# Late sort passes, group sizes and clear widths in a scatter-add kernel

## The chip, the cores and the metric

The kernel runs on one core of one Trainium2 chip. The metric is the device time of one launch in microseconds (us). The engines are PE (matmuls), PEld (its weight loads), DVE (elementwise work on vectors), ACT (activations and copies), POOL (here mostly the issuing of DMAs) and SP (issuing DMAs). Each engine takes its own instructions in order and waits on semaphores for the others.

## The reference

```python
N, E, D = 4096, 262144, 256
self_out = nodes @ w_self
src_feat = nodes[edges_src]          # E x D
msg = src_feat @ w_msg
agg = np.zeros((N, D)); np.add.at(agg, edges_dst, msg)
return self_out + agg
```

The edges are drawn once at random (uniform sources and destinations), the same draw each time.

## The kernel before

The kernel does not gather rows. It uses that the sum over edges is A @ (nodes @ w_msg), where A[dst, src] counts edges. `Y = nodes @ w_msg` is made once; A is made piece by piece in PSUM by matmuls of one-hot matrices and is multiplied by Y.

**Sort.** Every edge becomes a key: a destination segment (11 segments of SW = 374 destinations), then a source block (32 blocks of 128 sources), then the destination, then the source. One segment with one block is a *run* (NRUN = 352). DVE sorts the 262144 keys nearly, with a fixed list of compare-exchange passes (`SORT_A`, then 16 last passes `SORT_S`, each a minimum and a maximum). The sorted keys are cut into 2048 *chunks* of 128. The first 1024 chunks are the early half, the other 1024 the late half (HALF = 1024). Of the late half the 32 instructions of `SORT_S` are put off (`sort.late`): they run on DVE between the groups of the counting loop.

**Counting loop** (line 560 on). For each chunk one matmul adds e^T d into a PSUM bank: e is 128 edges by 128 sources, one-hot; d is 128 edges by W = 110 destinations, one-hot, at a column offset that PE reads from a register (`poff`). The offset is where the chunk's lowest destination lies in its run (`dl`). DVE makes e and d for a *group* of chunks at a time (`onehots`, list `sizes`): one subtraction `e_off` (L396), eight comparisons `e_oh` (L402), then `d_off` and seven `d_oh`. Each tile of one-hots has three buffers, so DVE may be up to three groups ahead.

**Ring.** The runs use six PSUM banks in turn. Before a run, `clear(r)` writes zeros with one matmul into GAP columns at each end of the SW + W = 484 columns of its bank; the columns between must then be covered by the chunks' windows. After a run ACT evicts the bank to SBUF as bf16 (L481); the last 110 columns, which belong to the start of the next run, are added to that run's tile by a DMA that POOL issues (`merge`, L501, two runs at a time), or are multiplied by an extra matmul (L519). 46 chunks later three matmuls (L524) multiply the run by its block of Y. At the end of a segment ACT copies the result and SP stores it in 12 pieces, one for every second eviction (L611).

**Late half.** Once its passes are done (chunk LATE_SUB), `late.bases()` finds each late chunk's lowest destination on DVE, `late.subtract` makes relative keys, `turn_late(0)` and `turn_late(1)` transpose them on PE through a bank slot of the ring that is set aside at run SHIFT (the second at chunk LATE_TURN), with an activation on ACT after each, and `late.places()` computes the offsets. `split_vals` then splits the values for the one-hots of chunk 1024 on.

**Order.** The order of everything up to `order.__exit__` is written out by hand. The check after it (L615 on) is placed among it by the scheduler: each half's `k16` is stored to a small DRAM row `kd` and loaded again shifted by one chunk as `kn`, both on SP's queue; `gn`, `v`, `bad` on DVE compare neighbours; a matmul (L642) sums them, and the result decides whether a plain loop (`_any_edges`) does the work anew.

The late passes go into the loop by this piece of before:

```python
if c >= LATE_FROM:
    for _ in range(LATE_STEP):
        if rest:
            rest.pop(0)()
if c == LATE_SUB:
    assert not rest
    late.bases()
```

Of the kernel before, what the change touches and what calls it, by code (L numbers as in the profile page):

```python
# [16 lines left out]
ALU = mybir.AluOpType  # L17
# [3 lines left out]
BW = 512  # L21
SW = 374
W = 110
GAP = W - 8
NB = 32
JB = 16
HALF = 1024
SHIFT = 148
LATE_FROM = 256
LATE_STEP = 4  # L30
LATE_SUB = 768
LATE_TURN = 872
LATE_USE = 960
NSEG = 11
NRUN = NSEG * NB
OFF = 6 * (NB - 1)
# [47 lines left out]
def kernel(  # L84
# [14 lines left out]
    NCOL = E // P  # L99
# [28 lines left out]
    tss = nc.vector.tensor_single_scalar  # L128
    tt = nc.vector.tensor_tensor
    stt = nc.vector.scalar_tensor_tensor  # L130
# [50 lines left out]
    for (c0, c1), (d64, s64) in zip(PIECES, ld):  # L181
        dlo = d64[:].bitcast(I32)[:, 0::2]
        slo = s64[:].bitcast(I32)[:, 0::2]
        c = slice(c0, c1)
# [3 lines left out]
            out=seg[:, c], in_=dlo, func=ACTF.Copy, scale=1.0 / SW, bias=0.5 / SW - 6.5  # L188
        )
        loaded = nc.scalar.activation(  # L190
            out=blk[:, c], in_=slo, func=ACTF.Copy, scale=1.0 / P, bias=0.5 / P - 0.5
# [62 lines left out]
    sort = _Sort(nc, tc, psum_sort, XA, (XS, XL), id2, zw)  # L254
    own = sort.run(plan, halo, project)

    def col16(name, dt):
        return meta.tile([P, G16], dt, name=name)

    k16, kmin, kn, rho, rhoc, gi, gn, dl, sl, wr, poff = (  # L260
        col16(n, I32)
        for n in ("k16", "kmin", "kn", "rho", "rhoc", "gi", "gn", "dl", "sl", "wr", "poff")
    )
# [7 lines left out]
    class Half:  # L271
# [47 lines left out]
        def places(self):  # L319
# [6 lines left out]
            if self.h == 0:  # L326
                stt(
                    out=sl[:, c], in0=rhoc[:, c], scalar=float(SHIFT - OFF), in1=sl[:, c],
                    op0=ALU.is_ge, op1=ALU.add,
# [44 lines left out]

    split_at = {0: 64, 64: 512, 512: HALF, HALF: HALF + 256, HALF + 256: NCOL}

    sizes = [8, 8, 16, 32, 32, 32] + [64] * ((NCOL - 128) // 64)
    assert sum(sizes) == NCOL

    def onehots(c, n):  # L380
# [32 lines left out]
    def clear_at(r):  # L413
        return min(max(line(at, r) for at in CLEAR[0:3]), line(CLEAR[3], r))

    def evac_at(r):
        return min(line(at, r + 1) for at in EVAC)
# [6 lines left out]
    def count_mm(ap, lhsT, rhs, start, after=()):  # L424
        mm = nc.tensor.matmul(  # L425
            out=ap, lhsT=lhsT, rhs=rhs, start=start, stop=True, skip_group_check=True,
        ).ins
        tc.declare_no_dep(
            mm, group="evac", keep=after, reason="disjoint banks by static schedule"
        )  # L430
        for i in after:
            tc.add_manual_dep(mm, i.name, DEP, reason="bank free")
        tc.add_to_no_dep_group("count", mm)
        last_mm[0] = mm
        return mm

    def bank(r):
        return (r + (r >= SHIFT)) % RING * BW

    def bank_free(slot):  # L440

        old = slot - RING
        if old == SHIFT:
            return [late_read[-1]]
        return [evac_of[old - (old > SHIFT)]] if old >= 0 else []

    late_read = []

    def turn_late(t):
        b = bank(SHIFT - 1) // BW  # L450
        b = (b + 1) % RING * BW
        mms, act = late.turn(t, ring[:, b:b + BW])
        for m in mms:
            after = bank_free(SHIFT) if t == 0 else [late_read[-1]]
            tc.declare_no_dep(
                m.ins, group="evac", keep=after, reason="disjoint banks by static schedule"
            )
            for i in after:
                tc.add_manual_dep(m.ins, i.name, DEP, reason="bank free")
            tc.add_to_no_dep_group("count", m.ins)  # L460
        ins = act.ins
        tc.declare_no_dep(
            ins, group="count", keep=[m.ins for m in mms], reason="disjoint banks by static schedule"
        )
        tc.add_manual_dep(ins, mms[-1].ins.name, DEP, reason="transposed")
        tc.add_to_no_dep_group("evac", ins)
        late_read.append(ins)

    def clear(r):
        b = bank(r)  # L470
        after = bank_free(r + (r >= SHIFT))
        zone = bass.AP(
            tensor=ring.tensor, offset=ring[:, b:b + 1].offset,
            ap=[list(ring[:].ap[0]), [SW + W - GAP, 2], [1, GAP]],
        )
        count_mm(zone, zer[:, 0, :], zer[:, 1:3, 0:GAP], True, after)

    def evac(r):
        at = ats[r % NAT]
        b = bank(r)  # L480
        ins = nc.scalar.copy(out=at[:, 0:SW + W], in_=ring[:, b:b + SW + W]).ins  # L481
        tc.declare_no_dep(
            ins, group="count", keep=[last_mm[0]], reason="disjoint banks by static schedule"
        )
        tc.add_manual_dep(ins, last_mm[0].name, DEP, reason="run complete")
        tc.add_to_no_dep_group("evac", ins)
        evac_of[r] = ins
        at_of[r] = at
# [4 lines left out]
    def by_dma(r):  # L493
        return r < NRUN - 8 and r // 2 % 6 > 0

    def merge(r):

        i, j = r % NAT, (r + 1) % NAT
        pairs = [(i, j, 2)] if j + 2 <= NAT else [(i, j, 1), (j, 0, 1)]
        for a, b, n in pairs:  # L500
            nc.gpsimd.dma_start(  # L501
                out=atr[:, b:b + n, 0:W], in_=atr[:, a:a + n, SW:SW + W], accum_op=ALU.add
            )
# [45 lines left out]
    if True:  # L549
        todo = []  # L550
        regs = []
        ncl = 0
        nev = 0
        rest = sort.late
        starts = {}
        c = 0
        for n in sizes:
            starts[c] = n
            c += n
        for c in range(NCOL):  # L560
            if c in starts:
                c0 = c
                if c == LATE_USE:
                    late.places()
                e, d = onehots(c, starts[c])
                if c >= LATE_FROM:
                    for _ in range(LATE_STEP):
                        if rest:
                            rest.pop(0)()
                if c == LATE_SUB:  # L570
                    assert not rest
                    late.bases()
                    for t in range(2):
                        late.subtract(t)
            if c == LATE_TURN:
                turn_late(1)
                late.total()
            ci = c - c0
            while ncl < NRUN and clear_at(ncl) <= c:
                if ncl == SHIFT:  # L580
                    turn_late(0)
                clear(ncl)
                ncl += 1
            if c % 8 == 0:
                regs = [nc.tensor.alloc_register(f"po{c}_{i}") for i in range(8)]
                q, h8 = c % HALF // G8, c // HALF * G8
                nc.tensor.load(regs, poff[q:q + 1, h8:h8 + 8])
            addr = nc.tensor.snap(
                regs[c % 8], donate=True, min_val=PSUM0, max_val=PSUM0 + 4 * (RING * BW - W)
            ).with_bounds(  # L590
                min_val=PSUM0, max_val=PSUM0 + 4 * (RING * BW - W),
                guaranteed_mod_val=0, out_of_modulus=4,
            )
            off = (addr - PSUM0) // 4
            count_mm(
                ring[:, bass.ds(off, W)], e[:, ci // 2, :, ci % 2], d[:, ci // 2, :, ci % 2], False
            )
            for _ in range(FILL.get(c + 1, 0)):
                nc.tensor.matmul(  # L599
                    out=out_ps[:, 2:4, :], lhsT=zw[:, 0:P], rhs=zw[:], start=True, stop=True,  # L600
                    skip_group_check=True,
                )
            while nev < NRUN and (evac_at(nev) <= c or c == NCOL - 1):
                evac(nev)
                if nev % 2 == 0 and nev and by_dma(nev - 1):
                    merge(nev - 2)
                todo.append((c + LAG + (SWITCH if nev % NB == 0 else 0), nev))
                if nev % 2 and stores:
                    dst, src = stores.pop(0)
                    tc.add_manual_dep(  # L610
                        nc.sync.dma_start(dst, src).ins, evac_of[nev].name, DEP, reason="pace"  # L611
                    )
                nev += 1
            while todo and (todo[0][0] <= c or c == NCOL - 1):
                apply_run(todo.pop(0)[1])  # L615
# [3 lines left out]
    bad = meta.tile([P, G16], FP32, name="bad")  # L619
    v = meta.tile([P, G16], FP32, name="v")  # L620
# [7 lines left out]
    for h in range(2):  # L628
# [4 lines left out]
    tss(out=gn[:], in_=kn[:], scalar=7, op=ALU.arith_shift_right)  # L633
    tt(out=bad[:], in0=rho[:], in1=rhoc[:], op=ALU.not_equal)
    tt(out=v[:], in0=gn[:], in1=gi[:], op=ALU.subtract)
    stt(out=bad[:], in0=v[:], scalar=float(GAP), in1=bad[:], op0=ALU.is_gt, op1=ALU.add)
    stt(
        out=bad[0:1, 0:1], in0=gi[0:1, 0:1], scalar=float(GAP - 1 - SW * OFF), in1=bad[0:1, 0:1],
        op0=ALU.is_gt, op1=ALU.add,
# [358 lines left out]
```

## Time and profile before

| | |
|---|---|
| median of 6 runs | 483.83 us (482.06 to 485.62) |
| profiled execution, its own time | 482.41 us |
| its span, first to last instruction | 480.6 us |
| mean granted clock of PE | 0.961 |
| busy: PE, DVE, ACT, POOL | 376.9, 416.0, 240.6, 196.3 us |
| first count matmul, last count matmul | 167.02, 469.51 us |
| clear matmuls of 128x204 | 352 of them, mean 251 ns each |
| late passes (XL, L746) | 32 of them, 28.1 us busy |

Times in the trace are us from the span's start. A line of a timeline gives start, length, engine, line of the kernel, operation, the tiles written and read with their shapes, and the number of like instructions; in brackets stand the idle time before and what ended it. Matmuls overlap in the array, so that the distance between two starts, not the length of one, is what a matmul costs PE. The page's span and the profiled execution's own time differ by what lies around the first and the last instruction.

### The profile page before, as it was taken

How to read it: one execution, taken by the hardware profiler on the slowest of the kernel's cores; microseconds unless marked ns; L12 is line 12 of the kernel's file. 1: busy time of each engine (PE TensorE's matmuls, PEld its weight loads, DVE VectorE, ACT ScalarE, POOL GpSimd, SP SyncE). 2: the span in 40 equal slices, each digit the busy share in tenths (PEclk: the TensorE clock that was granted, in tenths of full speed). 3: DMA queues.
4: the chain of work that ended last, by engine and by line, in shares of the span. 5: the costliest groups of instructions: out<-in, count | busy, mean ns of one | idle time of the engine just before them, and what ended most of it. 6: DMA issues, size and time to landing. Idle time of an engine off the chain costs nothing.

```text
span 480.6 us, 10985 instructions
## 1 busy us (share of the span) xinstructions
PE 376.9 (78%) x4098; PEld 309.2 (64%) x4107; DVE 416.0 (87%) x884; ACT 240.6 (50%) x459; POOL 196.3 (41%) x190
## 2 busy tenths in 40 slices
PE   0009636989872798987987997899998999999994
PEld 0004231655441368986877987789997999898893
DVE  8999999899899999999999998999987797987400
ACT  3100010321282245775555666677776777677771
POOL 4200000000000035765554566477666676766760
PEclk9999986999997799999899999999999999999998
DMA  8794111111000013343333334344544454544451
GB/s 324 114 165 131 25 26 25 28 25 25 14 0 0 2 14 26 30 51 38 28 41 38 32 30 54 37 47 48 49 45 49 40 57 37 56 38 53 38 60 40
DMA packets 66307, 23.78 MB, mean 49 GB/s; under 512 B 52171, under 2 KB 64971, under 8 KB 66251
## 3 DMA queue, kind: packets, MB, share of 16 engines
q0 software_dynamic: 43872, 10.42, 26.7%
q1 hardware_dynamic: 21548, 10.42, 8.2%
q10 hardware_dynamic: 830, 2.20, 1.2%
q8 instruction: 34, 0.56, 0.5%
q14 instruction: 23, 0.18, 0.1%
HBM read 8.92 MB, written 6.30 MB: 32 GB/s over the span
## 4 chain that ended last, share of the span: by engine, by line
DVE 42%; PE 34%; POOL 7%; issue 7%; DMA 6%; ACT 2%; SPq 0%; DVEq 0%; POOLq 0%; ACTq 0%
DVE XA L749 16%; PE ring L425 13%; PE out_ps L524 11%; DVE e_oh L402 7%; POOL atr L501 7%; DVE d_oh L402 6%; DVE XS L749 6%; PE warm L786 5%; DMA atr<-atr 4%; DVE XL L746 4%; PE tp_sw L892 2%; DMA d<-in_edges_dst_dram 2%; DVE d_off L396 1%; DVE e_off L396 1%; PE out_ps L599 1%
## 5 line engine op out<-in xcount | busy, mean ns | idle before, releaser
L501 POOL DMA_DIRECT2D atr<-atr x163 | 187.6, 1263 | 261.6 <-ACT atr L481 259.2
L481 ACT CAST atr<-ring 128x484 bf16<-128x484 f32 x352 | 192.4, 565 | 103.0 <-PE ring L425 82.7
L425 PE MATMUL ring<-d_oh,e_oh 128*128 128x110 bf16 x2048 | 195.5, 215 | 19.9 <-DVE d_oh L402 16.7
L425 PEld LDWEIGHTS <-e_oh 128*128 128x128 bf16 x2048 | 163.6, 98 | 24.9 <-issue 15.3
L524 PE MATMUL out_ps<-Y,atr 128*128 128x256 bf16 x1056 | 171.5, 274 | 2.2 <-DMA atr<-atr 1.9
L402 DVE TENSOR_SCALAR e_oh<-e_off 128x1024 bf16<-128x1024 int16 (+1 forms) x264 | 99.6, 448 | 19.5 <-PE ring L425 17.3
L786 PE MATMUL warm<-zw 128*128 128x512 bf16 x169 | 54.3, 416 | 67.4 <-DVE XA L749 51.9
L749 DVE TENSOR_TENSOR XA<-XA 128x510 f32<-128x510 f32 (+35 forms) x142 | 97.1, 732 | 5.3 <-ACT XA L896 3.6
L524 PEld LDWEIGHTS <-atr 128*128 128x128 bf16 x1056 | 90.4, 97 | 9.3 <-DMA atr<-atr 2.6
L425 PE MATMUL ring<-zer 128*128 128x204 bf16 x352 | 88.3, 251 | 1.5 <-ACT atr L481 1.3
L402 DVE TENSOR_SCALAR d_oh<-d_off 128x1024 bf16<-128x1024 int16 (+3 forms) x231 | 86.0, 442 | 1.1
L786 PEld LDWEIGHTS <-zw 128*128 128x128 bf16 x176 | 16.7, 102 | 101.1 <-issue 54.8
L896 ACT COPY XA<-tp_sw 128x512 f32<-128x512 f32 x24 | 14.2, 592 | 92.4 <-PE tp_sw L892 91.7
L425 PEld LDWEIGHTS <-zer 128*128 128x128 bf16 x352 | 34.3, 98 | 9.6 <-issue 6.0
L749 DVE TENSOR_TENSOR XS<-XS 128x512 f32<-128x512 f32 (+17 forms) x40 | 28.9, 769 | 2.6 <-ACT XS L950 2.0
L746 DVE TENSOR_TENSOR XL<-XL 128x1196 f32<-128x1196 f32 (+15 forms) x32 | 28.1, 919 | 0.3
L892 PEld LDWEIGHTS tp_sw<-XA,id 128*128 128x128 f32 x192 | 22.4, 190 | 4.6 <-issue 2.4
L892 PE MATMUL tp_sw<-XA,id 128*128 128x128 f32 x192 | 23.8, 276 | 1.9 <-DVE XA L749 1.7
L396 DVE TENSOR_TENSOR e_off<-slo_b,jrow 128x1024 int16<-128x1024 int16 (+1 forms) x33 | 21.6, 655 | 0.0
L396 DVE TENSOR_TENSOR d_off<-rel_b,drow 128x1024 int16<-128x1024 int16 (+1 forms) x33 | 21.5, 653 | 0.0
L643 DVE COPY bsum<-ring 1x3 f32<-1x3 f32 x1 | 0.1, 149 | 24.4 <-PE ring L642 24.4
L519 PE MATMUL out_ps<-Y,atr 128*128 128x256 bf16 x65 | 17.6, 271 | 0.0
(104 smaller groups left out, 153.9 us busy)
## 6 DMA issues: line engine op xcount, KB each, us to landing
atr<-atr POOLq DMA_DIRECT2D x123, 55.0 KB, 2.8
out_dram<-o_sb SPq DMA_DIRECT2D x110, 32.0 KB, 1.6
nodes_bf<-in_nodes_dram POOLq DMA_DIRECT2D x1, 2048.0 KB, 16.4
nodes_bf_dram<-nodes_bf SPq DMA_DIRECT2D x1, 2048.0 KB
atr<-atr POOLq DMA_DIRECT2D x40, 27.5 KB, 2.9
s<-in_edges_src_dram ACTq DMA_DIRECT2D x2, 512.0 KB
d<-in_edges_dst_dram SPq DMA_DIRECT2D x2, 512.0 KB, 8.2
XT<-nodes_bf_dram SPq DMA_TRANSPOSE x64, 2.4
```

The source lines that it names most:

```text
L396: tt(out=u[:, 0:n // 2], in0=v.to_broadcast(shp), in1=row[:, 0:JB, :].unsqueeze(1).to_broadcast(shp), op=ALU.subtract,)
L402: tss(out=o[:, 0:n // 2, j:j + w, :], in_=u[:, 0:n // 2, 0:w, :], scalar=float(-j), op=ALU.is_equal,)
L425: mm = nc.tensor.matmul(out=ap, lhsT=lhsT, rhs=rhs, start=start, stop=True, skip_group_check=True,).ins
L481: ins = nc.scalar.copy(out=at[:, 0:SW + W], in_=ring[:, b:b + SW + W]).ins
L501: nc.gpsimd.dma_start(out=atr[:, b:b + n, 0:W], in_=atr[:, a:a + n, SW:SW + W], accum_op=ALU.add)
L519: nc.tensor.matmul(out=out_ps[:, 0, :], lhsT=spill[:, SW:SW + P], rhs=Y[:, b, :], start=False, stop=False, skip_group_check=True,)
L524: nc.tensor.matmul(out=out_ps[:, t, :], lhsT=at[:, t * P:(t + 1) * P], rhs=Y[:, b, :], start=False, stop=(b == NB - 1), skip_group_check=True,
L746: self.defer.append(lambda: self.nc.vector.tensor_tensor(out=out, in0=in0, in1=in1, op=op))
L749: self.nc.vector.tensor_tensor(out=out, in0=in0, in1=in1, op=op),
L786: self.nc.tensor.matmul(out=w[:], lhsT=self.zw[:, 0:P], rhs=self.zw[:], start=True, stop=True).ins
L892: self.nc.tensor.matmul(out=tp[:, g * P:(g + 1) * P], lhsT=self.turned(rots[8 * h + 4 * t + g]), rhs=sel(x)[:, 4 * t + g], start=True, sto ...
L896: self.nc.scalar.copy(out=sel(y)[:, 4 * t:4 * t + 4], in_=tp[:].rearrange("p (g i b) -> p g i b", g=4, b=bb),)
```

## The change

Three things change together.

1. The late passes start at chunk 352 in place of 256 and end by chunk 896 in place of 768; how many follow a group depends on how far the loop is, not on a fixed four per group. Bases and subtractions follow at 896, the two turns come at run 165 (chunk 957) and chunk 970, and the places at chunk 1024.
2. Groups of 32 chunks reach to chunk 320 in place of 128, and four more stand behind chunk 1024, where there were groups of 64.
3. The clearing matmul covers 90 columns at each end in place of 102, and the check that the windows cover a run is written for steps inside a run and for its ends separately.

```diff
-GAP = W - 8
+GAP = 90
-SHIFT = 148
-LATE_FROM = 256
-LATE_STEP = 4
-LATE_SUB = 768
-LATE_TURN = 872
-LATE_USE = 960
+SHIFT = 165
+LATE_FROM = 352
+LATE_SUB = 896
+LATE_TURN = 970
...
-    sizes = [8, 8, 16, 32, 32, 32] + [64] * ((NCOL - 128) // 64)
+    sizes = [8, 8, 16] + [32] * 9 + [64] * 11 + [32] * 4 + [64] * 14
...
-        rest = sort.late
+        ops, done = sort.late, 0
...
-                if c == LATE_USE:
+                if c == HALF:
                     late.places()
                 e, d = onehots(c, starts[c])
                 if c >= LATE_FROM:
-                    for _ in range(LATE_STEP):
-                        if rest:
-                            rest.pop(0)()
+                    due = len(ops) * (c + starts[c] - LATE_FROM) // (LATE_SUB - LATE_FROM)
+                    for op in ops[done:due]:
+                        op()
+                    done = max(done, min(due, len(ops)))
                 if c == LATE_SUB:
-                    assert not rest
+                    assert done == len(ops)
...
-    stt(out=bad[:], in0=v[:], scalar=float(GAP), in1=bad[:], op0=ALU.is_gt, op1=ALU.add)
+    stt(out=bad[:], in0=v[:], scalar=float(W), in1=bad[:], op0=ALU.is_gt, op1=ALU.add)
+    tt(out=v[:], in0=v[:], in1=dl[:], op=ALU.add)
+    stt(out=bad[:], in0=v[:], scalar=float(SW + GAP), in1=bad[:], op0=ALU.is_gt, op1=ALU.add)
+    tss(out=v[:], in_=v[:], scalar=float(SW), op=ALU.is_ge)
+    stt(out=v[:], in0=dl[:], scalar=float(SW - GAP), in1=v[:], op0=ALU.is_lt, op1=ALU.mult)
+    tt(out=bad[:], in0=bad[:], in1=v[:], op=ALU.add)
```

## Prediction

> **What bounds the kernel now.** I read the share of the chain that ended last, then the busy time of each engine by stretch, then who waited for whom, then the timelines of DVE, PE and SP around the places where the bound changes.
>
> ```profile
> DVE 42%; PE 34%; POOL 7%; issue 7%; DMA 6%; ACT 2%; SPq 0%; DVEq 0%; POOLq 0%; ACTq 0%
> ```
> Two engines carry the end. The stretches (columns: length, then busy us of PE, PEld, DVE, ACT, POOL, then clock) show where one hands over to the other:
> ```profile
> 205.00:301.00 96.00, 81.46 (x1028) 74.72 (x1026) 92.68 (x195) 57.77 (x110) 55.54 (x50) 0.96 0.40 39
> 301.00:347.00 46.00, 43.79 (x573) 40.29 (x573) 45.05 (x121) 32.89 (x61) 29.60 (x26) 1.00 0.45 45
> 347.00:469.50 122.50, 118.54 (x1560) 109.51 (x1558) 84.78 (x204) 87.83 (x165) 83.61 (x73) 1.00 0.47 47
> ```
> Until 301 us DVE is full and PE has holes; after 347 us PE is full and DVE has holes. The waits from 165 to 302 us say what PE lacked, and that DVE itself waited once, for a DMA:
> ```profile
> PE ring L425 <- DVE d_oh L402: 16.7, 10, 3.1
> DVE gn L633 <- DMA kn<-kd: 1.7, 1, 1.7
> ```
> The last wait of PE for one-hots is at chunk 832, at 301.35 us. Chunk 896 starts at 311.91 us, though its one-hots were done at 307.96: from 301.35 on, PE sets the end. So work taken off DVE counts only if it lies ahead of the last such wait, and work taken off PE only behind it. The count matmuls of chunks 896, 960 and 1152 start at 311.91, 320.91 and 346.15, the last at 469.51.
>
> **The change part by part.** *Six small groups for three big ones.* Chunks 128 to 319 come in 32s in place of 64s. In DVE's timeline (start, length) a small group is one e_off, 8 e_oh, one d_off, 7 d_oh of half the width:
> ```profile
> 173.86 0.42 DVE L396 TENSOR_TENSOR e_off<-slo_b,jrow 128x512 int16<-128x512 int16 x1
> 174.38 2.22 DVE L402 TENSOR_SCALAR e_oh<-e_off 128x512 bf16<-128x512 int16 x8
> ...
> 178.92 0.41 DVE L396 TENSOR_TENSOR e_off<-slo_b,jrow 128x512 int16<-128x512 int16 x1
> ...
> 182.93 0.68 DVE L396 TENSOR_TENSOR e_off<-slo_b,jrow 128x1024 int16<-128x1024 int16 x1
> ```
> The three small groups of before take 4.01 (169.48 to 173.49), 5.06 (173.86 to 178.92) and 4.01 us, a mean of 4.36; the middle one met three DMA issues of POOL. The three big ones take 21.32 us together (182.93 to the first pass at 204.25). Six small ones: 26.16, so +4.84 us on DVE, while DVE is the bound (ends +2.7 by 4.01 and +9.0 by 5.06; I take the mean, as the merges that POOL issues go on).
> [...]
>
> *Passes spread.* The 32 passes keep their lengths; they begin behind group 384, in place of 256, and the last four (280.54 to 283.11, 2.57 us) come behind the one-hots of 832. The bases and subtractions (290.21 to 292.66, 2.45 us) and with them the check's gn and v (0.30) and gn's wait go behind the one-hots of 896, since kn is loaded from what the bases give. In before this reads:
> ```profile
> 291.45 1.29 DVE L300 SCALAR_TENSOR_TENSOR XL<-XL,gi 128x512 f32<-128x512 f32 x2
> 292.66 0.68 DVE L396 TENSOR_TENSOR e_off<-slo_b,jrow 128x1024 int16<-128x1024 int16 x1
> 295.09 0.18 DVE L633 TENSOR_SCALAR gn<-kn 128x16 int32<-128x16 int32 x1 [1.74 <-DMA kn<-kd]
> ```
> DVE point by point. One-hots of 832: 301.29 + 4.84 - 2.57 - 2.45 - 1.74 - 0.30 = 299.1. One-hots of 896: + 2.57 passes + 6.67 (its row, 301.29 to 307.96) = 308.3. PE goes from 832 to 896 in 10.56 us now, 8.2 without the eight transposes (0.9) and the wait for ACT (1.46 start to start) that move away, so it is there at 307.3 and waits: DVE stays the bound past 896. One-hots of 960: 308.3 + 2.45 + 1.74 + 0.30 + 7.40 (its row, 309.45 to 316.85) = 320.2 before any longer wait of gn, 0.7 earlier than PE starts 960 today. So nearly all that the later passes give back (7.06) is taken by the small groups (4.84) and by bases and wait that now lie ahead of the last wait.
>
> *gn's wait behind SP's queue.* kd is stored and kn loaded by SP, in order with the output stores:
> ```profile
> 291.24 0.35 SPq L625 DMA_DIRECT2D kd<-k  x1
> 292.66 0.82 SPq L629 DMA_DIRECT2D kn<-kd  x2
> 293.57 18.04 SPq L611 DMA_DIRECT2D out_dram<-o_sb  x16
> ```
> There the round trip ended before the stores of the segment began; each store waits for an eviction, one per two runs, 11.7 chunks or 1.55 us of PE. These stores belong to chunks 814 to 943, so at PE's chunk 896 to 915 the round trip stands among them, at two places, the store of kd and the loads of kn, half a spacing each on average: +1.55 us (ends 0 and 3.1). Behind gn on DVE wait the one-hots of 960, and PE for them. One-hots of 960: 321.8.
>
> *PE's hole and clock.* PE would be ready for 960 at 308.3 + 8.4 (a third of 25.24, the 192 chunks from 960) + 0.45 for four transposes = 317.2, a hole of 4.6 us (3.0 without SP). Holes of before, and the clock behind the first two (seventh column):
> ```profile
> 228.07 0.44 PE L425 MATMUL ring<-d_oh,e_oh 128*128 128x110 bf16 x3 [3.15 <-DVE d_oh L402]
> 260.80 0.21 PE L425 MATMUL ring<-d_oh,e_oh 128*128 128x110 bf16 x1 [2.81 <-DVE d_oh L402]
> 249.72 0.21 PE L425 MATMUL ring<-d_oh,e_oh 128*128 128x110 bf16 x1 [2.33 <-DVE d_oh L402]
> ```
> ```profile
> 228.00:231.50 3.50, 3.43 (x26) 2.90 (x26) 3.47 (x5) 1.12 (x2) 1.19 (x1) 0.51 0.00 0
> 262.20:265.60 3.40, 3.40 (x29) 2.94 (x28) 3.29 (x7) 1.59 (x4) 0.00 (x0) 0.50 0.00 0
> ```
> 2.81 and 3.15 us each brought about 3.4 us at half clock, 2.33 none. There it hid behind DVE; at 960 PE is the bound next, so it costs 1.7 us (ends 0 and 1.7; I take 1.7).
> [...]
>
> *The turn.* Its second half goes from chunk 872 to 970, so PE from 960 to 1152 takes 25.24 + 0.45 + 1.30 (idle for ACT, at 309.88 in before) + 1.7 - 0.3 (33 clears) = 28.4, to 350.2. DVE now waits with split_vals(1024) for it, and behind that the one-hots of 1024 and then PE: chunk 970 at 321.8 + 1.3 + 1.0 (half clock) = 324.1, turn to the end of ACT 1.34 (306.77 to 308.11) + 0.4, split 0.26, four small groups 17.44, a big one 7.1: 1152 at 350.6, PE there at 350.2. Those two are level, so nothing is gained between them. Chunk 1024 itself has room: one-hots at 330.5, PE at 333.6. The places (1.57 us, 307.88 to 309.45) and the checks' five more instructions of 128x16 (0.2 each) lie in DVE's wait for the turn and cost nothing; without that cover 1 to 2.6 us.
>
> *Clears.* Starts of a matmul and the next are 51 ns apart at 110 columns, 86 at 204, 109 at 256. Twenty-four columns fewer: 8.9 to 10.6 ns, I take 10. Behind 1152 lie 153 clears: -1.5 us. The 166 ahead of 960 lie where DVE sets the pace: 0. The evictions, which ACT makes 0.16 us behind PE, keep their 484 columns.
>
> **Sum.** 350.6 - 346.15 = +4.4, less 1.5: +2.9 us. On the profiled execution's 482.41 that is 485.3; the median of the runs stands 1.42 above that execution, so 483.83 + 2.9 = 486.7.
>
> **Rivals.** *Faster: DVE is rid of the wait.* If gn is placed later on DVE, into the wait for the turn, 960 is ready at 318.4, the hole is 1.2 us and the clock stays: PE 318.4 + 26.7 = 345.1, DVE 318.4 + 1.3 + 1.34 + 0.26 + 17.44 + 7.1 = 345.9, less 1.5: -1.8 us; with small groups at 4.01 DVE is 2.1 earlier by 960 and 1152 starts at 343.0: -4.7. It is faster from the point where a small group costs under 4.25 us and gn waits under half a us. For it: two of three small groups took 4.01. Against: the order that put gn behind the e_off just behind the bases has the same data to go by. About -3.3: 480.5.
> *No change.* No delay from SP and a wait of 1.74 as now: with the half clock 1152 starts at 349.0 and the sum is +1.3; without it +0.1 or less. About 484.5.
> *Much slower.* Small groups all like the 5.06 one: 4.2 more before 896 and 2.8 more behind 1024, +9.9: 493.7. Against: only one of three met so many issues.
> *It doesn't do what it says.* If an end were not covered by 90 columns, the kernel would go into its loop over single groups of 128 edges, some 2048 rounds, far beyond any range here. Following the list of exchanges on the drawn edges by plain array arithmetic, the first window of a run starts at most 76 columns in (90 allowed) and the last at 291 or later (284 needed): under 1 in 100.
>
> **How the numbers follow.** About 0.5% (2.4 us) is what a measurement of this kernel tells from no change. Forecast 0.41 and the much slower case 0.04, together slower 0.45. No change: 0.35. Faster: 0.20, of which half under 480.5. Range 480.5 to 490.5: from the middle of the faster case to the forecast with the upper end for SP (+1.55) and small groups at 4.6 (+2.3).
>
> **What would show it.** Right: PE's last wait for d_oh moves from chunk 832 to 960 and 1152, near 321 and 350 us; gn waits 1.7 us or more on kn among output stores; the clock is 0.5 for 3.4 us behind a hole of over 2.8; clears of 128x180 start about 76 ns ahead of the next matmul; from 1152 to the last count matmul it takes 121.8 us in place of 123.36. Wrong: if DVE is ahead of PE at 896, or 960 starts before 319.

## The result and the profile after

The changed kernel takes 485.1 us in the median (481.99 to 487.8), the kernel before, run beside it, 482.52 us: a ratio of 1.0051, interval 1.0035 to 1.0066, so 2.5 us slower (1.7 to 3.2). The prediction was 2.9 us slower. Measured again beside three experiments it came to 1.0044 (1.0019 to 1.0069).

The stretches of the profile after, cut where its bound changes (length, then busy us of PE, PEld, DVE, ACT, POOL, then the clock):

```profile
205.00:308.30 103.30, 87.41 (x1111) 79.54 (x1108) 101.48 (x221) 61.78 (x115) 61.06 (x54) 0.97 0.39 38
308.30:349.50 41.20, 36.74 (x451) 33.61 (x451) 36.44 (x131) 27.17 (x50) 23.44 (x21) 0.92 0.42 45
349.50:473.10 123.60, 119.83 (x1570) 110.22 (x1570) 91.69 (x223) 87.99 (x165) 84.03 (x73) 0.99 0.47 47
```

DVE is full up to 308 us and PE waits for it, where before that was so up to 301. PE is full only from 349.5 on; before, from 301 to 347, both engines were nearly full (43.79 and 45.05 of 46.00 us). The stretch between, here 36.74 and 36.44 of 41.20 us, belongs to neither engine alone: there the two wait for each other.

The waits of the profile after from 165 to 470 us, and the last three of them for one-hots in PE's timeline, at chunks 896, 960 and 1152:

```profile
PE ring L423 <- DVE d_oh L400: 20.0, 13, 4.1
DVE gn L632 <- DMA kn<-kd: 2.7, 1, 2.7
```
```profile
308.33 0.26 PE L423 MATMUL ring<-d_oh,e_oh 128*128 128x110 bf16 x2 [1.34 <-DVE d_oh L400]
320.38 0.43 PE L423 MATMUL ring<-d_oh,e_oh 128*128 128x110 bf16 x3 [3.49 <-DVE d_oh L400]
349.54 0.21 PE L423 MATMUL ring<-d_oh,e_oh 128*128 128x110 bf16 x1 [0.82 <-DVE d_oh L400]
```

PE's last wait for one-hots has moved from chunk 832 to 1152. The points of the prediction's sum against this execution: one-hots of 832 at 299.1 (PE starts at 298.85), of 896 at 308.3 (308.33), of 960 at 321.8 (320.38), chunk 1152 at 350.6 (349.54), the last count matmul 121.8 us behind it (123.5, at 473.06).

In SP's queue, what stood in doubt. First a line of before, then after:

```profile
205.89 67.86 SPq L611 DMA_DIRECT2D out_dram<-o_sb  x27
```
```profile
203.47 83.47 SPq L610 DMA_DIRECT2D out_dram<-o_sb  x36
309.22 0.36 SPq L624 DMA_DIRECT2D kd<-k  x1
310.64 1.66 SPq L628 DMA_DIRECT2D kn<-kd  x2
312.40 17.55 SPq L610 DMA_DIRECT2D out_dram<-o_sb  x13
```

The round trip of kd and kn stands ahead of the segment's output stores, not among them, though PE is past chunk 896 by then and, by the code, the first stores are due at chunk 814. The stores stood behind it, and the segment's twelve left within 5.5 us afterwards. A segment has twelve stores, so the 36 ahead of kd are three whole segments. In before there are 27, two segments and three stores of the third: it was there that kd stood among a segment's stores, and nine of them stood behind it, the first leaving at 293.57.

### The profile page after: what moved, and what is told of

It is laid out like the page before. It is cut to its first block, busy times and chain, and to the rows that moved or that the text cites. A ratio compares the mean times of both kernels' runs of the same rounds, so it can differ in the third digit from the quotient of the medians.

```text
span 484.2 us, 11081 instructions
## 1 busy us (share of the span) xinstructions
PE 379.8 (78%) x4098; PEld 310.0 (64%) x4107; DVE 423.1 (87%) x974; ACT 240.8 (50%) x459; POOL 196.7 (41%) x190
## 4 chain that ended last, share of the span: by engine, by line
DVE 51%; PE 36%; DMA 5%; issue 3%; ACT 2%; POOL 1%; SPq 0%; DVEq 0%; ACTq 0%; POOLq 0%
DVE XA L753 13%; PE ring L423 13%; PE out_ps L522 12%; DVE e_oh L400 12%; DVE d_oh L400 10%; PE warm L790 7%; DVE XS L753 6%; DVE XL L750 5%; PE tp_sw L896 2%; DVE d_off L394 2%; DMA d<-in_edges_dst_dram 2%; DMA atr<-atr 2%; DVE e_off L394 2%; PE out_ps L511 1%; PE out_ps L517 1%
## 5 line engine op out<-in xcount | busy, mean ns | idle before, releaser
L522 PE MATMUL out_ps<-Y,atr 128*128 128x256 bf16 x1056 | 173.5, 276 | 0.4 <-DMA atr<-atr 0.2
L400 DVE TENSOR_SCALAR e_oh<-e_off 128x1024 bf16<-128x1024 int16 (+1 forms) x304 | 102.4, 408 | 14.3 <-PE ring L423 11.2
L522 PEld LDWEIGHTS <-atr 128*128 128x128 bf16 x1056 | 91.4, 98 | 10.4 <-issue 2.9
L400 DVE TENSOR_SCALAR d_oh<-d_off 128x1024 bf16<-128x1024 int16 (+3 forms) x266 | 88.5, 403 | 1.3
L423 PE MATMUL ring<-zer 128*128 128x180 bf16 x352 | 85.5, 243 | 0.1
L517 PE MATMUL out_ps<-Y,atr 128*128 128x256 bf16 x65 | 18.0, 276 | 1.5 <-issue 1.5
```

Source lines behind the costliest of these rows:

```text
L400: tss(out=o[:, 0:n // 2, j:j + w, :], in_=u[:, 0:n // 2, 0:w, :], scalar=float(-j), op=ALU.is_equal,)
L423: mm = nc.tensor.matmul(out=ap, lhsT=lhsT, rhs=rhs, start=start, stop=True, skip_group_check=True,).ins
L517: nc.tensor.matmul(out=out_ps[:, 0, :], lhsT=spill[:, SW:SW + P], rhs=Y[:, b, :], start=False, stop=False, skip_group_check=True,)
L522: nc.tensor.matmul(out=out_ps[:, t, :], lhsT=at[:, t * P:(t + 1) * P], rhs=Y[:, b, :], start=False, stop=(b == NB - 1), skip_group_check=True,
```

## The experiments

Unless said otherwise a difference in us is the ratio's distance from 1, times 483, against the kernel before on the same chip. Half the interval is 1 to 2.5 us, and differences between two experiments are less sure than either.

**The clears alone.** Kernel before with

```diff
-GAP = W - 8
+GAP = 90
```
and the new check.

> Kernel before with the 90-column clears and the new check alone. Theory A (the sum of the prediction): only the 200 or so clears behind chunk 832, where PE sets the end, count, at 10 ns each: 1.5 to 2.0 us faster than before. Rival C (the profile of after took 123.5 us from chunk 1152 to the last count matmul against 123.4 of before, so the narrower clears give nothing there): the same time as before, within 0.5 us. In its profile A wants the start of a clear and the next matmul 76 ns apart.

Ratio 0.9975 (0.9939 to 1.0012): 1.2 us faster, with an interval that holds zero, so the median alone doesn't decide between theory A and rival C. The start of a clear and of the next matmul are 77 ns apart against 87 (medians of the 153 clears behind chunk 1152), so the slot shrank as expected. In its profile the way from 1152 to the last count matmul takes 121.3 us against 123.4.

**The early small groups alone.** Kernel before with

```diff
-    sizes = [8, 8, 16, 32, 32, 32] + [64] * ((NCOL - 128) // 64)
+    sizes = [8, 8, 16] + [32] * 9 + [64] * 27
```

> Kernel before with groups of 32 chunks up to chunk 320 alone. Theory A: six small groups cost DVE 4 to 5 us more than three big ones, and DVE is the bound up to chunk 832, so the one-hots of 832 come 4 to 5 us later and the whole is 4 to 5 us slower than before. Rival B (small groups cost nothing at the end, since PE starts sooner on each): within 1 us of before.

Ratio 1.0084 (1.0051 to 1.0117), 4.1 us slower (2.5 to 5.7). PE's last wait for one-hots in its timeline is still at chunk 832, now at 306.00:

```profile
306.00 0.26 PE L425 MATMUL ring<-d_oh,e_oh 128*128 128x110 bf16 x2 [1.09 <-DVE d_oh L402]
```
This is 4.65 us later than before. That small groups cost nothing at the end (rival B) falls.

**The early groups back at 64.** Kernel after with

```diff
-    sizes = [8, 8, 16] + [32] * 9 + [64] * 11 + [32] * 4 + [64] * 14
+    sizes = [8, 8, 16, 32, 32, 32] + [64] * 14 + [32] * 4 + [64] * 14
```

> Kernel after with the groups of chunks 128 to 319 put back to 64; the four small ones behind 1024 stay. Theory A: DVE reaches every point from chunk 320 on 4 to 5 us sooner, the hole of PE ahead of 960 keeps its length, so 4 to 5 us faster than after and about 2 us faster than before. Rival B: the loss is the wait of gn with the clock drop alone, so this stays 2 to 3 us slower than before.

Ratio 0.9882 (0.9835 to 0.9929): 5.7 us faster than before, some 8 us faster than after, where 4 to 5 was expected. In the profiles chunk 896 starts 4.8 us sooner (303.5 against 308.3) and 1152 4.9 us sooner (344.6). The rest lies behind 1152 (121.2 us against 123.5 in the first profile of after), where nothing was edited; the second profile of after has 121.3 there too. So the mechanism stands, and what goes beyond some 5 us isn't explained.

**gn held until the places.** Kernel after with this edit, shortened here:

```diff
-    tss(out=gn[:], in_=kn[:], scalar=7, op=ALU.arith_shift_right)
+    tc.add_manual_dep(tss(out=gn[:], ...).ins, placed[-1].ins.name, DEP, reason="after the places")
```
where `placed` holds the last instruction of each `places()`.

> Kernel after with gn (and so the check behind it) held until the places are done, so that its wait for kn lies where DVE waits for the turn. Theory A: the one-hots of 960 come 2.7 to 3.1 us sooner, PE's hole there shrinks from 3.5 to about 0.5 us, the half clock of 6.8 us behind it is gone (3 us), together 4.5 to 5.5 us faster than after, some 2 to 3 us faster than before. Rival D (the half clock behind the hole costs nothing): 2.7 us faster than after, the same as before.

Ratio 0.9978 (0.9944 to 1.0012): 1.1 us faster than before and some 3.5 us faster than after. gn waits 0.03 us, PE's hole at 960 is 1.39 us and no half clock follows. But from 960 to 1152 it still takes 29.8 us against 29.2 in after with its half clock. DVE begins the split for 1024 as late behind the start of chunk 960 as in after, 3.66 us against 3.65. In after it waited there for the turn, which the half clock held up (its four transposes took 1.07 us there, 0.61 here):

```profile
324.02 0.23 DVE L370 TENSOR_SCALAR slo_b<-vals 128x256 int16<-128x256 int16 x1 [0.91 <-ACT vals L310]
```
Here it waits for nothing, but the check's instructions stand ahead of it (320.28 to 322.39). So this run can't tell what the clock is worth; it does show that PE was not what set the pace, since PE waits 1.15 us for the one-hots of 1152. This led to theory A2, that behind 960 DVE's chain of turn, split, four small groups and one big one does.

**The late passes alone.** Kernel after with GAP, the check and the group sizes of before.

> Kernel before with the late passes, bases, turns and places moved as in the change, and nothing else: its group sizes and its clears of 102 columns. The prediction's sum without the six small groups ahead (4.84) and the clears: one-hots of 960 at about 317, with the half clock 1152 at 345.4: 0.7 us faster than before. Theory A2, formed from the run with the first groups back at 64 (960 started at 314.6, and from there to 1152 it was DVE's chain of four small groups, not PE, that set the pace): without the small groups behind 1024 PE sets the pace from 960 on, 1152 at about 342.6, so 3 to 4.5 us faster than before.

Ratio 0.9924 (0.9897 to 0.995), 3.7 us faster (2.4 to 5.0). This is A2's figure and not the 0.7 of the prediction's sum. The profile says otherwise: chunk 960 starts at 317.2 and 1152 at 345.3, as the sum had it (317 and 345.4), where A2 wanted 342.6. But the profiled execution is the slowest of the eleven (482.12 us), and it holds the longest gn wait of all, 3.8 us:

```profile
DVE gn L632 <- DMA kn<-kd: 3.8, 1, 3.8
```
From there to 1152 it takes 28.2 us with big groups, 1.0 to 1.8 us less than in the profiles of after and of the two experiments above that keep the small ones, although half clock is on for 2.8 us of it, and PE waits for no one-hots at 1152. That the other executions are faster because gn waits less in them is likely, not shown.

**The hole filled.** Kernel after with 24 matmuls of zeros behind chunk 959, into a column block that nothing reads:

```diff
+            for _ in range(WARM.get(c + 1, 0)):      # WARM = {960: 24}
+                nc.tensor.matmul(out=out_ps[:, 3, :], lhsT=zw[:, 0:P], rhs=zw[:, 0:D], start=False, ...)
```

> Kernel after with 24 matmuls of zeros into an unused column block between chunks 959 and 960, 2.6 us of PE work in the hole of 3.5 us, so that the clock stays full. The prediction's step (the half clock costs PE 1.7 us or more): 1.7 to 3 us faster than after. Theory A2 (behind 960 DVE's chain sets the pace, and the half clock only delays the turn that it waits for): 0.5 to 1.2 us faster than after. Nothing at all would say that the check's instructions on DVE cover the turn.

Ratio 0.9975 (0.9947 to 1.0002): 1.2 us faster than before, 3.3 to 3.7 us faster than after, which looks like the clock's price. The profile doesn't bear that out. PE's and the other engines' columns from 960 to 1152 and from there to the last count matmul, first here, then in after:

```profile
320.90:349.80 28.90, 26.04 (x339) 23.54 (x337) 27.64 (x106) 20.45 (x38) 17.41 (x15) 1.00 0.40 40
349.80:468.90 119.10, 117.01 (x1570) 109.03 (x1570) 91.63 (x223) 87.96 (x165) 83.84 (x73) 1.00 0.49 48
```
```profile
320.38:349.54 29.16, 28.17 (x337) 25.65 (x337) 27.30 (x106) 20.56 (x38) 17.35 (x15) 0.90 0.40 40
349.54:473.06 123.52, 119.78 (x1570) 110.18 (x1569) 91.66 (x223) 87.99 (x165) 84.03 (x73) 0.99 0.47 47
```
The clock is full (1.00 against 0.90), and the stretch where it was low is 0.3 us shorter. The gain lies behind 1152, where the clock was no issue but for 3.4 us of the first profile of after. What makes it is open; the clock in the hole is not shown to be it. The 119.1 us are the least of the ten profiles with narrow clears, which reach from there to 123.5 us though the loop behind 1152 is nearly the same in them (only the check moves), so that one profile of each kernel says little about this stretch.

**Old sizes, late passes, narrow clears, check at the end.** Kernel after with the sizes of before, and gn tied to the last one-hot instruction in place of the last places.

> Late passes and 90-column clears as in the change, group sizes of before, and gn with the check behind it held until the last one-hots. Theory A2: one-hots of 960 at about 312.5, level with PE, no hole and no half clock, PE sets the pace from there, 1152 at about 339, 1.5 us less from the clears: 7 to 9 us faster than before. If small groups behind 1024 are needed to cover the turn, PE would wait for the one-hots of 1024 and gain 2 us less.

Ratio 0.9858 (0.9824 to 0.9892): 6.9 us faster than before (5.2 to 8.5), at 477.15 us. It beats both kernels. DVE's timeline at the split for 1024 and PE's at chunks 896 and 960:

```profile
317.05 0.23 DVE L370 TENSOR_SCALAR slo_b<-vals 128x256 int16<-128x256 int16 x1 [1.50 <-ACT vals L310]
317.19 0.22 DVE L371 TENSOR_SCALAR rel_b<-vals 128x256 int16<-128x256 int16 x1
317.33 0.69 DVE L396 TENSOR_TENSOR e_off<-slo_b,jrow 128x1024 int16<-128x1024 int16 x1
```
```profile
304.41 0.26 PE L425 MATMUL ring<-d_oh,e_oh 128*128 128x110 bf16 x2 [0.27 <-DVE d_oh L402]
314.03 0.32 PE L425 MATMUL ring<-d_oh,e_oh 128*128 128x110 bf16 x3 [0.48 <-DVE d_oh L402]
```
At 896 and 960 PE waits 0.27 and 0.48 us, and DVE has 1.5 us to spare ahead of the split: both engines arrive together. From 960 to 1152 it takes 27.4 us.

**The same with four small groups behind 1024.**

> The same with the change's four small groups behind chunk 1024. Theory A2: DVE's chain from 960 to 1152 sets the pace again, 1152 at about 342: 5 to 6.5 us faster than before, some 2 us slower than with groups of 64 there. The rival (the small groups behind 1024 cover the turn): at least as fast as with groups of 64.

Ratio 0.9879 (0.9842 to 0.9916): 5.8 us faster. The stretch from 960 to 1152 takes 28.6 us against 27.4, with a wait of 1.15 us for one-hots at 1152. In the medians the two can't be told apart.

**After again, and after with big groups behind 1024.** The first is the changed kernel itself; the second has `[8, 8, 16] + [32] * 9 + [64] * 27`.

> The changed kernel itself once more, beside the next three on the same chip. Expected as measured first, 2 to 3.5 us slower than before; its profile tells which of the waits of the first profile come again: PE's wait for one-hots at 960 (3.5 us) and 1152 (0.8) should, the wait at chunk 1264 (1.5 us) with the half clock behind it should not if it was chance.

> Kernel after with groups of 64 behind chunk 1024, the nine small ones ahead stay. Theory A2: behind 960 PE sets the pace in place of DVE's four small groups, there is no wait for one-hots at 1152, 1 to 2 us faster than after. Rival (the small groups cover the turn): PE waits 1 us or more for the one-hots of 1024, and it is not faster than after.

After came to 1.0044, the second to 1.0039 (1.0013 to 1.0065), so no difference in the medians. In the profiles the stretch from 960 to 1152 is 29.4 against 28.0 us, and the wait at 1152 is gone. PE is not kept waiting at 1024, so the small groups there cover nothing; that they cost 1 to 1.4 us is seen in profiles only. Of after's first profile the waits at 960 (3.00 us now) and 1152 (0.82) came again, the one at chunk 1264 (1.5 us, ended at 365.94) did not.

**The check held until the end.** Kernel after with gn tied to the last one-hot instruction.

> Kernel after with gn and all of the check behind it held until the last one-hots. Theory A2: one-hots of 960 come 2 to 3 us sooner, the split for 1024 waits for the turn's activation and not for the check, 1152 starts 2.5 to 3.5 us sooner, so 2.5 to 3.5 us faster than after, about level with before or 1 us faster. Where gn was held only until the places it was some 3.6 us faster than after; if the check on DVE ahead of the split cost something there, this is up to 0.7 us faster still.

Ratio 0.9989 (0.996 to 1.0018), 2.7 us faster than after beside it. DVE's split now waits for the turn alone, and PE's hole at 960 is 1.06 us:

```profile
319.48 0.17 DVE L335 TENSOR_SCALAR poff<-poff 128x8 int32<-128x8 int32 x1
321.14 0.23 DVE L370 TENSOR_SCALAR slo_b<-vals 128x256 int16<-128x256 int16 x1 [1.49 <-ACT vals L310]
```
The split begins 3.01 us behind chunk 960's start, and from 960 to 1152 it takes 28.7 us, against 3.66 and 29.8 with gn behind the places. In the medians it is not the faster of the two (0.5 and 1.1 us faster than before), so what the check's instructions cost ahead of the split is seen in the profiles only.

**Wide clears in after.**

> Kernel after with clears of 102 columns at each end and the check of before. Theory A: only the clears behind 1152 count, 1.5 to 2 us slower than after, 4 to 5 us slower than before. Rival C: the same as after.

Ratio 1.0037 (1.0007 to 1.0068), no slower than after with 1.0044. The slot is 87 ns again, yet from 1152 on it takes 121.7 us against 121.3 and 123.5 in the two profiles of after. Here the clears' 1.5 us did not show.

## Why the prediction was right, point by point

The path was right: DVE stays the bound past chunk 896, and the small groups take back what the later passes give. Two terms stood on reasons that the runs don't bear out, gn's wait and the half clock, and the gain by the clears isn't settled.

*Small groups.* The term was 26.16 us for six. The profile after, DVE's timeline at the first and behind the last of them:

```profile
182.16 0.42 DVE L394 TENSOR_TENSOR e_off<-slo_b,jrow 128x512 int16<-128x512 int16 x1
...
208.58 0.67 DVE L394 TENSOR_TENSOR e_off<-slo_b,jrow 128x1024 int16<-128x1024 int16 x1
```
That is 26.42 us, so 5.1 us more than the three big ones of before. Taken alone it cost 4.1 us in the median (2.5 to 5.7). Right, and the mean of three rows was the row to take: the six took 4.21 to 4.66 us, none as much as 5.06.

*Later passes.* The way up to 896 came out to 0.3 us. That DVE stays the bound past 896, and that bases and gn thereby land ahead of the last waits, is shown by chunk 960: held back, gn gave 2.7 to 3.5 us.

*gn's wait.* The size was near, the reason wrong. The step put the round trip among the output stores and took 1.55 us for that. The trace has it ahead of them, between two segments, and it is before, read in the prediction as free of stores, that had it among them, with a wait of 1.74 us. So a place among the stores does not by itself lengthen the wait. It was 2.74 us in the first profile and 1.84 in the second, so 1.0 and 0.1 us over the 1.74 of before. Over the ten profiles with gn at its old place the wait ranged from 1.55 to 3.75 us. In the first profile of after the issue of the second kn load alone took 1.27 us against 0.43 in before; in the one with 3.75 us it took 0.44, so that isn't the only cause. What makes it vary is open; no run shows a delay by stores, which the 1.55 us stood for.

*Half clock.* It came, as the holes of before suggested, and twice as long in the first profile:

```profile
319.50:322.90 3.40, 2.52 (x19) 2.33 (x19) 3.19 (x20) 1.12 (x2) 1.19 (x1) 0.50 0.00 0
322.90:326.40 3.50, 3.50 (x26) 2.84 (x25) 2.45 (x13) 2.94 (x5) 0.39 (x1) 0.51 0.25 23
```
In the second profile, with a hole of 3.00 us, it was 3.4 us. But the 1.7 us in the sum was mis-sized: with the hole filled and the clock full the stretch from 960 to 1152 was 0.3 to 0.5 us shorter. DVE's chain set the pace there, which the prediction saw as level with PE (350.6 against 350.2) and not as leading. In every profile with four small groups behind 1024 PE waits 0.5 to 1.15 us for the one-hots of 1152, and in none with big ones. What the half clock costs goes through the turn: the split begins 3.65 us behind chunk 960 in both profiles of after, and 3.01 us with the hole filled or gn at the end.

That 2.81 us and more bring the drop and 2.33 us don't, as the prediction read it, was wrong too: holes of 2.83 us (clears alone, ahead of chunk 576) and 2.86 us (late passes, four small groups behind 1024, check at the end, ahead of 576) brought none, while one of 1.95 us (late passes alone, ahead of 704) did. In before and in after the starts of the drops behind chunk 128 lie whole numbers of 3.413 us apart (228.04 and 262.17 in before: 10; 217.13, 247.85, 319.53 and 367.31 in after: 9, 21 and 14). Cut into windows of this length from the drops of its own profile, the time around four holes reads, of before (2.81 us), of the clears alone (2.83 us), of the late passes alone (1.95 us) and of after, the window at half clock behind 3.49 us:

```profile
258.76:262.17 3.41, 1.37 (x19) 1.30 (x19) 3.38 (x9) 0.46 (x1) 1.10 (x1) 1.00 0.49 42
```
```profile
257.76:261.17 3.41, 1.78 (x26) 1.70 (x26) 3.38 (x7) 0.71 (x2) 0.70 (x1) 1.00 0.40 29
```
```profile
272.17:275.58 3.41, 1.46 (x21) 1.27 (x18) 3.41 (x8) 0.86 (x3) 2.19 (x2) 1.00 0.61 54
```
```profile
319.53:322.94 3.41, 2.56 (x19) 2.38 (x19) 3.17 (x21) 1.12 (x2) 1.19 (x1) 0.50 0.00 0
```
PE is busy for 40% of the first window and half clock follows; for 52% of the second and none follows; for 43% of the third and it follows. From chunk 128 to the last one before and after have 157 such windows at full clock. Half clock follows the six with PE busy, as the profile models it, for 46% or less, and none of the 151 with 50% or more. So in these windows PE's busy share goes with what follows, and the length of a hole of 2 to 3 us does not; what makes it so no run shows. The 6.8 us of the first profile of after are two windows: the first (the fourth line) has PE busy for 75% and another at half clock behind it. The other six at half clock in the two profiles have PE busy for 99% or more, and full clock behind them.

*The turn.* The split came at 324.02, 1.8 us ahead of the sum's 325.8, and 1.4 of this is the lead of chunk 960. The four small groups took 17.63 us and the big one 7.48, where the sum had 17.44 and 7.1.

*Clears.* The slot shrank by 10 ns as the sum had it. That 153 of them make 1.5 us at the end is not settled: 1.2 us (interval with zero) on the kernel before, nothing on the kernel after. From 1152 to the last count matmul the four profiles with wide clears take 123.1 us in the mean (121.7 to 123.9) and the ten with narrow ones 121.6 (119.1 to 123.5). That is the sum's 1.5 us, but in executions that differ by three times as much.

*The sum.* That its total hit so closely is in part luck, because errors of opposite sign met: chunk 960 came 1.4 us sooner than forecast, chunk 1152 1.1 us sooner, and the last 900 chunks took 1.7 us longer than forecast in the first profile. In the second the points lie closer, 321.84, 351.26 and the last at 472.52 against 321.8, 350.6 and 472.4, though that execution began its count matmuls 1.4 us later (168.07 against 166.71). Taken alone the three parts give +4.1, -3.7 and -1.2, together -0.8, while all of them without the four late small groups give +1.9. The gap of 2.7 us lies inside the joint interval of those four numbers (root of the sum of squares of 1.6, 1.3, 1.8 and 1.3: 3.0), so that parts hinder each other is not shown.

*Rivals.* Faster was where the wait is taken off DVE: the sum gave that 1.8 us below before, the run with gn behind the places 1.1. Of the no-change rival the condition, a wait as in before, held in the second profile (1.84 us), but chunk 1152 started at 351.26 and not at its 349.0. The much slower case did not come. The loop over single groups of edges was not entered, as the span shows.

## What to carry to other kernels

Where two engines alternate as the bound, list for each step on which side of the last wait it falls: the same late passes gained 3.7 us alone and were more than paid away by group sizes that cost 5 us of the bounding engine. Look first which engine makes the smaller groups: here half a group took DVE 4.2 to 4.7 us and a whole one 7.1, and DVE set the end. A check that nobody needs until the end belongs behind the last real work of its engine: ahead of it, the one-hots of 960 waited on DVE for the check's DMA, and holding it back gave 2.7 us.

## What was not expected of the hardware

The length of a hole of 2 to 3 us in PE did not tell whether half clock came: it came behind one of 1.95 us (late passes alone) and not behind one of 2.86 us (late passes, four small groups behind 1024, check at the end). In before and in after the drops behind chunk 128 start whole numbers of 3.413 us apart, and of the 157 windows of that length at full clock half clock followed the six with PE busy for 46% or less and none of the 151 with 50% or more. Behind the hole of 3.49 us in after two windows at half clock came back to back, 6.8 us, with PE busy for 75% of the first. The round trip of a small store and load through DRAM, from the store's issue to the instruction that reads, took from 3.70 us (small groups alone, 295.51 to 299.21) to 5.86 us (late passes alone, 304.98 to 310.84), and neither the stores around it nor one slow issue accounts for the difference.
